# A two-layer hybrid transformer block on Trainium2: the norms' statistics products emitted later and pinned in TensorE's order

## The chip, the cores and the metric

The kernel runs on one core of one Trainium2 chip. The metric is the device time of one execution in microseconds (us). TensorE is called PE below, its weight loads PEld, VectorE DVE, ScalarE ACT, GpSimd POOL, and the queue that issues the transfers SP. The three executions shown of the kernel before took 3201.49, 3206.51 and 3210.8 us.

## What is computed

Two layers over 1024 latent tokens and 256 context tokens of width 1024, in float32. The reference, cut to what matters here:

```python
def rmsnorm(x, g):
    xf = x.astype(jnp.float32)
    y = xf * lax.rsqrt(jnp.mean(xf * xf, axis=-1, keepdims=True) + EPS)
    return y.astype(x.dtype) * g
...
def trunk_layer(x, xc, mod, mod_c, p, ang_row, ang_col, last):
    ...
    h = rmsnorm(x, p["g_pre_mix"]) * (1 + sc1) + sh1
    hc = rmsnorm(xc, p["g_pre_mix"]) * (1 + sc1c) + sh1c
    u = h @ w_in
    ...
    y = jnp.concatenate([y_sc, y_mla, y_cf, y_na], axis=-1) @ p["w_out"]
    x = x + ga1 * rmsnorm(y, p["g_post_mix"])
    ...
    hm = rmsnorm(x, p["g_pre_mlp"]) * (1 + sc2) + sh2
    x = x + ga2 * rmsnorm(sq_relu_mlp(hm, p["w_mlp1"], p["w_mlp2"]), p["g_post_mlp"])
```

The four mixers are a short convolution, latent attention (MLA), a Conformer convolution with a layer norm, and neighbourhood attention. The second layer leaves the context tokens' own output out.

## The kernel before

Activations lie transposed, 128 features on the partitions and tokens along the free axis, in three segments (`SEGS`): latent tokens 0 to 511, latent 512 to 1023, context 256. A float32 product is made as three float32r products (`mm3`, L117 to L124) of a high and a low half, which ACT and DVE or POOL split off (`hilo`, L93 and L94).

A norm needs, for each token, the sum of squares over 1024 features, which lie on eight tiles and 128 partitions. ACT squares (L133, L210, L229 or L863), DVE adds the squares up (`fold`, L145 and L148), and `rstd` (L151 to L174) does the rest:

- the statistics products, L161: for each 128 tokens one product of the accumulated squares with a column of ones, into one or two to four columns of a PSUM bank;
- the square root on ACT (L164), the reciprocal on DVE (L165), and DVE's product of the identity with it (L167);
- the broadcast product, L170, which spreads the factors of up to 512 tokens over all partitions in the same bank;
- a copy to SBUF by ACT (L173), except for norms with `ptag="O"`, which keep the bank.

`modulate` (L176 to L194) then makes the input of a projection from it (DVE L192, ACT L193, DVE L194), and `norm` (L200 to L236) the residual step (DVE L223 and L225) and, where another norm follows, that one's squares and its `modulate`. Both are generators: they yield a cost after each piece.

PSUM has banks under four tags: G (two), S (three), T (two), O (one). Products that ask for "R" get S or G in rotation. In the attention stage of segment 0 the rotation is G alone, so that projections and the Conformer's statistics share the two G banks, while attention has S, T and O.

The order of the work comes from two places. `merge` (L954) interleaves generators: it runs a main one and lets the others spend `rate` cost units for each unit of the main one (`RATES`, L33). This gives the order in which instructions are written. A list scheduler then sets each engine's queue at build time: by its own estimate of when operands are there it may put an instruction ahead of earlier ones of its engine. On the chip each queue runs in that fixed order.

In `layer` (L973) the stages are: projections with the Conformer convolution; MLA's projections; `atta`, the attention of segment 0, merged with the remaining projections (`rest`) and `cf_post` (L407), whose layer norm uses `rstd` with tag G; the output projection of segment 0 (`outproj`, L849) merged with the first norm of `y0` and attention of the other segments (`attb`); the second half's norm `n2` merged with `attb` at rate `od`; the MLP (`mlp`, L871) of segment 0 with the rest of `attb`; the output projections and norms of `y1` and, in layer 0, of `y2` (256 context tokens); and the MLP of segments 1 and 2, whose products on the context wait for `y2`'s norm (`ready`, L909). Norms of `y1` and `y2` use tag O, with one bank.

Two switches stand in the way of this flow: `PD and next(n2)` and `next(nb)` emit the first piece of a norm, its statistics included, before the stage that it is merged with. `stats` (L1107) runs a generator's first two pieces.

```python
    def merge(main, *others):
        ...
        for c in main:
            done += c
            for i, (g, rate) in enumerate(others):
                while live[i] and spent[i] < done * rate:
                    ...
                        spent[i] += next(g)
```

Of the kernel before, what the change touches and what calls it, by code (L numbers as in the profile page):

```python
# [4 lines left out]
F32 = mybir.dt.float32  # L5
# [7 lines left out]
P = 128  # L13
# [11 lines left out]
NA_SCALE = 64 ** -0.5  # L25
NEG = -1e30
HB = 2
QTAG = 'xl'
PA, PD = 0, 1
WALT = (3, 2)  # L30
MPE, RM, MX = 7, 1.0, 4
ROT0, ROT1, ROT2 = 'SGSGS', 'SGSGS', 'SGSGS'
# [29 lines left out]
class Kern:  # L62
# [88 lines left out]
    def rstd(self, accs, width, n, ptag, tag="e2", keep=False):  # L151

        nc = self.nc
        nt = n // P
        ps = self.ps(ptag)
        for t in range(nt):
            for i, a in enumerate(accs):  # L160
                nc.tensor.matmul(ps[:, t:t + 1], a[:, t * P:(t + 1) * P], self.ones[:, 0:1], start=i == 0,  # L161
                                 stop=i == len(accs) - 1)
        r = self.t([P, 12], "sm")[:, :nt]
        nc.scalar.activation(r, ps[:, :nt], AF.Sqrt, bias=self.eps, scale=1.0 / width)  # L164
        nc.vector.reciprocal(r, r)  # L165
        s = self.t([P, nt, P], tag)
        nc.vector.tensor_tensor(s, self.ident[:, None, :].to_broadcast([P, nt, P]),  # L167
                                r[:, :, None].to_broadcast([P, nt, P]), op=ALU.mult)
        s = s.rearrange("p t c -> p (t c)")
        nc.tensor.matmul(ps[:, :n], self.ones, s, start=True, stop=True)  # L170
        if keep:
            return ps[:, :n]
        nc.scalar.activation(s, ps[:, :n], AF.Copy)  # L173
        return s  # L174

    def modulate(self, get, n, l, which, v, H, o, acc=None, ptag="R", tag="e2", tmp=None):  # L176

        nc = self.nc
        if acc is None:
            acc = self.sumsq([lambda k=k: get(k) for k in range(KT)], n, tag)
            yield n / 60
        rs = self.rstd([acc], D, n, ptag, tag, ptag == "O")
        yield n / 100
        A, sh = self.gains(l, "A" + which, v), self.gains(l, "s" + which, v)
        for k in range(KT):
            x = get(k)
            hi, lo = (h.k(k)[:, o:o + n] for h in (H() if callable(H) else H))  # L190
            t = self.ps(tmp)[:, :n] if tmp else x
            nc.vector.scalar_tensor_tensor(t, x, A[:, k:k + 1], rs, op0=ALU.mult, op1=ALU.mult)  # L192
            nc.scalar.activation(hi, t, AF.Identity, bias=sh[:, k:k + 1])  # L193
            nc.vector.scalar_tensor_tensor(lo, t, sh[:, k:k + 1], f32(hi), op0=ALU.add, op1=ALU.subtract)  # L194
            yield n / 400
# [4 lines left out]
    def norm(self, y, si, o, n, l, which, acc, xsrc, xdst, nxt=None, ptag="R", tag="e2", tmp=None):  # L200
# [6 lines left out]
        if acc is None:  # L207
# [2 lines left out]
                nc.scalar.activation(q, y.tiles[k // y.kk][:, k % y.kk:k % y.kk + 512 // n, o:o + n], AF.Square)  # L210
                acc = self.fold(acc, q, 512 // n, n, tag)
            yield n / 60
        rs = self.rstd([acc], D, n, ptag, tag, ptag == "O")
        yield n / 100
        acc = None
        g = 512 // n
# [15 lines left out]
        if nxt:  # L232
            l2, w2, H = nxt
            yield n / 200
            yield from self.modulate(yk, n, l2, w2, v, H, o, acc, ptag, tag, tmp)


    def mod_pe(self, load):
# [168 lines left out]
    def cf_post(self, l, segs):  # L407
# [5 lines left out]
        for si in segs:  # L413
            o, n = SEGS[si]
            cs = [cfy[j][:, o:o + n] for j in range(2)]
            ps = self.ps("R")[:, :n]
            for j in range(2):
                nc.tensor.matmul(ps, self.ones, cs[j], start=j == 0, stop=j == 1)
            yield 4.0
            sqs = []  # L420
            for c in cs:
                nc.vector.scalar_tensor_tensor(c, ps, -1.0 / 256, c, op0=ALU.mult, op1=ALU.add)
                q = self.t([P, n], "e2")
                nc.scalar.activation(q, c, AF.Square)
                sqs.append(q)
            yield 5.0
            rs = self.rstd(sqs, 256, n, "G")
            yield 8.0
            zs = []
            for j, c in enumerate(cs):  # L430
                nc.vector.tensor_tensor(c, c, rs, op=ALU.mult)
                nc.scalar.activation(c, c, AF.Silu, scale=vec[:, V_LNG + j:V_LNG + j + 1],
                                     bias=vec[:, V_LNB + j:V_LNB + j + 1])
            yield 3.0
            for j, c in enumerate(cs):
                zh = self.t([P, n], "ge", F32R)
                zl = self.t([P, n], "ge", F32R)
                self.hilo(zh, zl, c)
                zs.append((zh, zl))
            for m in range(2):  # L440
                po = self.ps("R")[:, :n]
                self.mm3(po, [(wh(2 * j + m), wl(2 * j + m), zs[j][0], zs[j][1])
                              for j in range(2)])
                nc.scalar.activation(cs[m], po, AF.Copy)
            yield 4.0
# [54 lines left out]
    def mla_project(self, l, H, segs, qsegs):  # L500
# [4 lines left out]
        def ckv(si, ps):  # L505
            o, n = SEGS[si]
            c = self.t([P, n], "e2")
            nc.scalar.activation(c, ps, AF.Copy)
            rs = self.rstd([self.sumsq([lambda: c], n)], P, n, "R")
            nc.vector.scalar_tensor_tensor(c, c, vec[:, V_GKV:V_GKV + 1], rs, op0=ALU.mult, op1=ALU.mult)  # L510
            self.hilo(nh[:, o:o + n], nl[:, o:o + n], c)

# [6 lines left out]
    def mla_heads(self, l, qsegs):  # L519
# [21 lines left out]
        wh, wl = self.weights(self.a["wuq"][l], D)  # L541
        for si in qsegs:
            o, n = SEGS[si]
            rs = self.rstd([self.sumsq([lambda j=j: cq[j][:, o:o + n] for j in range(2)], n)], 256, n, "R")
            yield n / 100
            qh, ql = self.t([P, 2, n], "ah", F32R), self.t([P, 2, n], "ah", F32R)
            for j in range(2):
# [425 lines left out]
    def layer(self, l, H, pend):  # L973
# [50 lines left out]
        self.merge(self.outproj(l, 0, 0, 256, y0), (attb, R['ob']))  # L1024
        HM[0] = self.newh(512)
        na = self.norm(y0, 0, 0, 256, l, "1", self.acc, xsrc, self.scr["XM"], (l, "2", HM[0]))
        PA and next(na)
        self.merge(self.outproj(l, 0, 256, 256, y0), (na, R['on']), (attb, R['oc']))
        self.walt = 0
        n2 = self.norm(y0, 0, 256, 256, l, "1", self.acc, xsrc, self.scr["XM"], (l, "2", HM[0]))  # L1030
        PD and next(n2)
        self.merge(ch(na, n2), (attb, R['od']))
        m0 = self.mlp(l, (0,), HM, "s", {0: "s"}, None)
        self.merge(self.upto(m0, "tail"), (attb, R['mb']))
# [12 lines left out]
        self.merge(self.outproj(l, 1, 256, 256, y1), (nb, 1.5))  # L1047
        self.go(nb)
        nb = self.norm(y1, 1, 256, 256, l, "1", self.acc, xsrc, self.scr["XM"], (l, "2", HM[1]), **free)
        next(nb)  # L1050
        if not last:
            for m in (0, 2, 1, 3):
                self.ysplit(2, m, "c5")
            y2 = Seg(self.pools["s"], 256, F32, "s", self.nm("yo"))
            self.merge(self.outproj(l, 2, 0, 256, y2), (nb, R['pm']))
            self.go(nb)
            HM[2] = self.newh(256)
# [5 lines left out]
        if last:  # L1063
# [2 lines left out]
            self.merge(self.upto(m, "part"), (resa, R['pr']))  # L1066
            self.go(resa)
            nb = self.norm(self.macc[1], 1, 0, 256, l, "2", None, self.scr["XM"], xout, **free)
            self.stats(nb)
            n2 = self.norm(self.macc[1], 1, 256, 256, l, "2", None, self.scr["XM"], xout, tag="pt", tmp="T")  # L1070
            self.go(m)
            self.stats(n2)
            self.go(nb, n2)
            return None
        vecs = self.mod_vectors(("c5", "ah"))
# [15 lines left out]
        hn = hn()  # L1091
        self.merge(self.upto(m, "part"), (nb, R['mn']), (hn, R['mc']))
        self.go(nb, hn)
        p1 = self.norm(self.macc[1], 1, 0, 512, l, "2", None, self.scr["XM"], xout, (1, "1", lambda: HN[1]), **free)
        self.stats(p1)
        self.merge(m, (p1, R['mt']))
        HN[1], HN[2] = self.newh(512), self.newh(256)
        pend = ch(p1, self.norm(self.macc[2], 2, 0, 256, l, "2", None, self.scr["XM"], xout, (1, "1", HN[2]), **free))
        return HN, pend

    def turn(self, rot):
# [2 lines left out]
        yield 0.0  # L1104

    @staticmethod
    def stats(g):  # L1107

        next(g)
        next(g)  # L1110

    def upto(self, m, mark):

# [174 lines left out]
```

## Time and profile before

| what | value |
|---|---|
| runs | 3201.49, 3206.51, 3210.8 us (median 3206.51) |
| the profiled execution | 3201.57 us, of it the span from first to last instruction 3199.6 us |
| PE busy | 2959.4 us (92%), mean granted clock 0.961 |
| PEld, DVE, ACT, POOL busy | 2534.7, 2019.0, 1399.5, 1076.6 us |
| HBM | 127 GB/s over the span |

Busy shares are averages over stages with different limits. Times below are us from the span's start; a row of the timeline merges neighbours of one kind and ends, in brackets, with the idle time of its engine before it and what ended it.

### The profile page before, as it was taken

The page shows a single profiled execution, that of the slowest core. Times are in us where ns is not written, and L with a number is a line of the kernel's source. Part 1 is how long each engine was busy: PE and PEld are TensorE (multiplying, and loading weights), DVE is VectorE, ACT ScalarE, POOL GpSimd, SP SyncE. Part 2 cuts the span into 40 slices and gives each one's busy share as a digit, 9 for nine tenths or more (in the row PEclk, how much of TensorE's full clock was granted, in tenths as well). Part 3 has the DMA queues.
Part 4 walks back from the last instruction along what each step waited for, and adds up shares of the span by engine and source line. Part 5 has one row for each costly group of instructions (what it writes and reads, how often), then busy time and mean ns, then how long its engine had stood idle before and what let it go on. Part 6 is the DMA issues. An engine that isn't in the chain of part 4 may idle for free.

```text
span 3199.6 us, 46244 instructions
## 1 busy us (share of the span) xinstructions
PE 2959.4 (92%) x15916; PEld 2534.7 (79%) x15916; DVE 2019.0 (63%) x4128; ACT 1399.5 (44%) x2882; POOL 1076.6 (34%) x861
## 2 busy tenths in 40 slices
PE   7879889979999989889999998998989999989997
PEld 5767668878888878768888887777878888978886
DVE  8999556685753377975543689556776633654335
ACT  3313445666553364212322443555765433543332
POOL 2302122225444432223333421222334444334443
PEclk9889889989999989999999999998989999999998
DMA  7435423453533354563212443425445333534233
GB/s 264 152 120 189 118 62 101 126 148 107 159 109 96 102 186 150 193 213 107 91 60 66 145 140 126 141 76 144 151 116 146 111 96 96 172 100 147 96 97 104
DMA packets 284461, 410.01 MB, mean 128 GB/s; under 512 B 28098, under 2 KB 129474, under 8 KB 284228
## 3 DMA queue, kind: packets, MB, share of 16 engines
q1 hardware_dynamic: 284228, 407.07, 40.9%
q8 instruction: 126, 2.06, 0.3%
q14 instruction: 107, 0.88, 0.1%
HBM read 354.66 MB, written 52.30 MB: 127 GB/s over the span
## 4 chain that ended last, share of the span: by engine, by line
PE 70%; DVE 9%; DMA 5%; ACT 2%; issue 2%; SPq 1%; POOL 0%; DVEq 0%; ACTq 0%; POOLq 0%
PE G L122 11%; PE G L123 11%; PE G L124 11%; PE S L122 9%; PE S L124 9%; PE S L123 9%; PE T L675 3%; DMA xl<-in_wmodt_dram 2%; PE O L688 1%; PE O L687 1%; DVE xl L288 1%; DMA ah<-KR 1%; PE S L809 1%; PE S L758 1%; PE S L759 1%
## 5 line engine op out<-in xcount | busy, mean ns | idle before, releaser
L94 POOL TENSOR_TENSOR wl<-raw,wh 128x512 fp32r<-128x512 f32 x672 | 898.4, 1340 | 1525.7 <-ACT wh L93 1399.1
L93 ACT ACTIVATE wh<-raw 128x512 fp32r<-128x512 f32 x768 | 483.0, 631 | 847.7 <-PE S L123 391.9
L122 PE MATMUL G<-h,wh 128*128 128x512 f32 (+1 forms) x1128 | 427.0, 379 | 6.5 <-ACT h L193 2.3
L123 PE MATMUL G<-h,wh 128*128 128x512 f32 (+1 forms) x1128 | 423.0, 375 | 4.4 <-DVE h L194 4.3
L124 PE MATMUL G<-h,wl 128*128 128x512 f32 (+1 forms) x1128 | 423.4, 375 | 0.2 <-POOL wl L94 0.2
L122 PE MATMUL S<-h,wh 128*128 128x512 f32 (+1 forms) x904 | 324.6, 359 | 2.9 <-ACT h L193 1.6
L124 PE MATMUL S<-h,wl 128*128 128x512 f32 (+1 forms) x904 | 324.7, 360 | 1.4 <-POOL wl L94 1.4
L123 PE MATMUL S<-h,wh 128*128 128x512 f32 (+1 forms) x904 | 323.7, 358 | 0.0
L659 POOL TENSOR_SCALAR ah<-ah,sm 128x1280 f32<-128x1280 f32 (+3 forms) x144 | 148.2, 1033 | 410.4 <-DVE sm L658 155.2
L929 DVE TENSOR_TENSOR ac<-ac,S 128x512 f32<-128x512 f32 (+1 forms) x340 | 208.9, 617 | 114.6 <-PE S L124 113.7
L122 PEld LDWEIGHTS G<-h,wh 128*128 128x128 f32 x1128 | 215.7, 191 | 46.0 <-ACT h L193 4.7
L123 PEld LDWEIGHTS G<-h,wh 128*128 128x128 f32 x1128 | 215.2, 191 | 42.2 <-DVE h L194 6.0
L124 PEld LDWEIGHTS G<-h,wl 128*128 128x128 f32 x1128 | 215.4, 191 | 36.4 <-issue 0.7
L94 DVE TENSOR_TENSOR pt<-T,pt 128x512 fp32r<-128x512 f32 (+1 forms) x280 | 169.3, 615 | 87.9 <-ACT pt L93 86.6
L929 DVE TENSOR_TENSOR ac<-ac,G 128x512 f32<-128x512 f32 (+1 forms) x268 | 169.0, 631 | 82.1 <-PE G L124 80.9
L93 ACT ACTIVATE pt<-T 128x512 fp32r<-128x512 f32 (+1 forms) x280 | 146.5, 543 | 117.5 <-PE T L675 103.4
L122 PEld LDWEIGHTS S<-h,wh 128*128 128x128 f32 x904 | 173.9, 192 | 29.5 <-ACT h L193 2.3
L124 PEld LDWEIGHTS S<-h,wl 128*128 128x128 f32 x904 | 173.6, 192 | 27.3 <-POOL wl L94 2.7
L123 PEld LDWEIGHTS S<-h,wh 128*128 128x128 f32 x904 | 173.9, 192 | 25.6
L122 PE MATMUL G<-s,wh 128*128 128x512 f32 (+1 forms) x534 | 185.3, 348 | 2.2 <-ACT ge L863 1.7
L124 PE MATMUL G<-s,wl 128*128 128x512 f32 (+1 forms) x534 | 182.0, 341 | 3.3 <-DVE wl L94 3.2
L123 PE MATMUL G<-s,wh 128*128 128x512 f32 (+1 forms) x534 | 182.0, 341 | 0.3 <-DVE s L94 0.3
(339 smaller groups left out, 6938.9 us busy)
## 6 DMA issues: line engine op xcount, KB each, us to landing
raw<-in_w_dram SPq DMA_DIRECT2D x520, 256.0 KB, 2.6
xl<-in_wmodt_dram SPq DMA_DIRECT2D x160, 256.0 KB, 3.0
raw<-in_wout_dram SPq DMA_DIRECT2D x144, 256.0 KB, 3.0
raw<-in_win_dram SPq DMA_DIRECT2D x96, 256.0 KB, 3.1
ah<-KN SPq DMA_DIRECT2D x32, 320.0 KB, 4.9
ah<-MV SPq DMA_DIRECT2D x16, 640.0 KB, 6.4
ah<-NV SPq DMA_DIRECT2D x16, 640.0 KB, 4.9
XM<-yo SPq DMA_DIRECT2D x36, 256.0 KB, 2.9
```

The costliest lines, as they stand in the source:

```text
L93: nc.scalar.activation(hi, src, AF.Copy)
L94: (eng or nc.vector).tensor_tensor(lo, src, f32(hi), op=ALU.subtract)
L122: nc.tensor.matmul(out, wh, xh, start=i == 0, stop=False)
L123: nc.tensor.matmul(out, wh, xl, start=False, stop=False)
L124: nc.tensor.matmul(out, wl, xh, start=False, stop=i == last)
L288: nc.vector.scalar_tensor_tensor(q, w, 1.0, vecs[v][h], op0=ALU.mult, op1=ALU.mult, accum_out=dst)
L659: nc.gpsimd.tensor_scalar(p[:, :L], p[:, :L], sm[:, 9:10], 1.0, op0=ALU.mult, op1=ALU.mult)
L675: nc.tensor.transpose(T[:, i, q * P:(q + 1) * P], ps_list[q][:, cols[q]:cols[q] + P], self.ident)
L687: nc.tensor.matmul(O[:, a:b], V[:, kt, :], th[:, i, a:b], start=first, stop=False)
L688: nc.tensor.matmul(O[:, a:b], V[:, kt, :], tl[:, i, a:b], start=False, stop=last)
L758: nc.tensor.matmul(S, Qt[:, 0, q:q + P], K[0][:, ks], start=True, stop=False)
L929: nc.vector.tensor_tensor(a, a, ps, op=ALU.add)
```

## The change

`rstd` becomes a generator. It yields `LEAD` = 6.0 units before it takes its PSUM bank and emits the statistics products, and `MID` = 3.0 units before the broadcast product. So in a merge other work is written between the squares and the statistics, and between statistics and broadcast. `pin` wraps both products: the scheduler must keep each behind the last PE instruction that was written before it; later ones may still go ahead of it. At three sites (`cf_post`, MLA's key/value norm, MLA's query norm) `value` runs the generator through without a break, so there only the pin is new. The early pieces (`PA`, `PD`, `next(nb)`) are gone; `stats` runs four pieces instead of two; the tail of the last layer merges the first half's norm with the last products; `y2` moves from the pool `s` to the pool `ah`; and `p1` and its successor keep tag `e2` instead of `pt`.

```diff
+LEAD, MID = 6.0, 3.0
-PA, PD = 0, 1
...
     def rstd(self, accs, width, n, ptag, tag="e2", keep=False):
...
         nt = n // P
+        yield LEAD
         ps = self.ps(ptag)
         for t in range(nt):
             for i, a in enumerate(accs):
-                nc.tensor.matmul(ps[:, t:t + 1], a[:, t * P:(t + 1) * P], self.ones[:, 0:1], start=i == 0,
-                                 stop=i == len(accs) - 1)
+                self.pin(nc.tensor.matmul(ps[:, t:t + 1], a[:, t * P:(t + 1) * P], self.ones[:, 0:1], start=i == 0,
+                                          stop=i == len(accs) - 1))
...
-        nc.tensor.matmul(ps[:, :n], self.ones, s, start=True, stop=True)
+        yield MID
+        self.pin(nc.tensor.matmul(ps[:, :n], self.ones, s, start=True, stop=True))
...
-        rs = self.rstd([acc], D, n, ptag, tag, ptag == "O")
+        rs = yield from self.rstd([acc], D, n, ptag, tag, ptag == "O")
...
+    def pin(self, ins):
+
+        return self.tc.keep_in_program_order(ins)
...
-            rs = self.rstd(sqs, 256, n, "G")
+            rs = self.value(self.rstd(sqs, 256, n, "G"))
...
-            rs = self.rstd([self.sumsq([lambda: c], n)], P, n, "R")
+            rs = self.value(self.rstd([self.sumsq([lambda: c], n)], P, n, "R"))
...
-        PA and next(na)
...
-        PD and next(n2)
...
-        next(nb)
         if not last:
...
-            y2 = Seg(self.pools["s"], 256, F32, "s", self.nm("yo"))
+            y2 = Seg(self.pools["ah"], 256, F32, "ah", self.nm("yo"))
...
-            self.stats(nb)
+            next(nb)
             n2 = self.norm(self.macc[1], 1, 256, 256, l, "2", None, self.scr["XM"], xout, tag="pt", tmp="T")
-            self.go(m)
-            self.stats(n2)
+            self.merge(m, (nb, 1.5))
+            self.go(nb)
             self.go(nb, n2)
...
-        p1 = self.norm(self.macc[1], 1, 0, 512, l, "2", None, self.scr["XM"], xout, (1, "1", lambda: HN[1]), **free)
-        self.stats(p1)
+        p1 = self.norm(self.macc[1], 1, 0, 512, l, "2", None, self.scr["XM"], xout, (1, "1", lambda: HN[1]), ptag="O", tmp="T")
+        next(p1)
```

How PE's queue changes at three places. First, `cf_post` in the attention stage of layer 0, where the Conformer's layer norm takes its statistics (bank `G_3964`) of segment 1. L675, L687, L688 and L758 to L760 are attention's products; L122 to L124 on a G bank are projections. Before:

```order
L123 MATMUL G_3800<-h_3_399,wh_3581 128x512
L124 MATMUL G_3800<-h_3_395,wl_3582 128x512
L161 MATMUL G_3964<-ones,e_3827 128x1
L161 MATMUL G_3964<-ones,e_3830 128x1
L161 MATMUL G_3964<-ones,e_3827 128x1
L161 MATMUL G_3964<-ones,e_3830 128x1
L161 MATMUL G_3964<-ones,e_3827 128x1
L758 MATMUL S_3450<-ah_3287,xl_3445 128x512
L687 MATMUL O_3176<-pt_3234,ah_2938 128x256
```

Now (lines from 155 on have moved down, attention's by six):

```order
L765 MATMUL S_3947<-ah_3929,xl_3934 128x256
L766 MATMUL S_3947<-ah_3926,xl_3934 128x256
L162 MATMUL G_3964<-ones,e_3827 128x1
L162 MATMUL G_3964<-ones,e_3830 128x1
L162 MATMUL G_3964<-ones,e_3827 128x1
L162 MATMUL G_3964<-ones,e_3830 128x1
L162 MATMUL G_3964<-ones,e_3827 128x1
L162 MATMUL G_3964<-ones,e_3830 128x1
L162 MATMUL G_3964<-ones,e_3827 128x1
L162 MATMUL G_3964<-ones,e_3830 128x1
L693 MATMUL O_3857<-pt_3863,ah_3641 128x256
L122 MATMUL G_4074<-h_0_400,wh_3575 128x256
```

The statistics stand behind 194 attention products that came after them before, and no projection stands among those 194: the next one on a G bank is the last row shown.

Second, the norm of `y1`'s second half in layer 0, which runs beside the output projection of `y2` (L122 to L124 on `c`). Before, the broadcast of the first statistics (L170) and the statistics of the second (L161) are neighbours:

```order
L124 MATMUL S_11907<-c_11642,wl_11904 128x256
L161 MATMUL O_11620<-ones,ma_11237 128x1 x2
L170 MATMUL O_11620<-pt_11626,ones 128x256
L161 MATMUL O_11772<-ones,pt_11696 128x1 x2
L170 MATMUL O_11772<-pt_11778,ones 128x256
L122 MATMUL S_11948<-c_11639,wh_11938 128x256
```

Now there are 42 products between the first two and 101 between the next two:

```order
L123 MATMUL G_11948<-c_11630,wh_11938 128x256
L162 MATMUL O_11719<-ones,ma_11237 128x1 x2
L124 MATMUL G_11948<-c_11630,wl_11939 128x256
...
L123 MATMUL S_11997<-c_11633,wh_11993 128x256
L172 MATMUL O_11719<-pt_11725,ones 128x256
L124 MATMUL S_11997<-c_11633,wl_11994 128x256
```

Third, the norm of `y2` just after, beside the first MLP products of segment 1 (L122 to L124 on `h`, second half of its columns). Before, 138 products stand between its broadcast `O_12085` (not shown) and the statistics that follow it:

```order
L124 MATMUL S_12491<-h_3_11194,wl_12428 128x256
L161 MATMUL O_12234<-ones,pt_12119 128x1 x2
L122 MATMUL S_12491<-h_3_11194,wh_12427 128x256
L123 MATMUL S_12491<-h_3_11198,wh_12427 128x256
L124 MATMUL S_12491<-h_3_11194,wl_12428 128x256
L170 MATMUL O_12234<-pt_12240,ones 128x256
L122 MATMUL G_12521<-h_0_12059,wh_12350 128x256
```

Now there is none:

```order
L122 MATMUL S_12463<-h_3_11194,wh_12384 128x256
L123 MATMUL G_12426<-h_3_11198,wh_12317 128x256
L124 MATMUL G_12426<-h_3_11194,wl_12318 128x256
L123 MATMUL S_12463<-h_3_11198,wh_12384 128x256
L124 MATMUL S_12463<-h_3_11194,wl_12385 128x256
L172 MATMUL O_12137<-pt_12143,ones 128x256
L162 MATMUL O_12418<-ones,pt_12215 128x1 x2
L172 MATMUL O_12418<-pt_12424,ones 128x256
L122 MATMUL G_12521<-h_0_12059,wh_12311 128x256
```

## Rows read from the trace of the kernel before

**Rows 1.** The page: busy time, then PE and its clock in 40 slices.
```profile
PE 2959.4 (92%) x15916; PEld 2534.7 (79%) x15916; DVE 2019.0 (63%) x4128; ACT 1399.5 (44%) x2882; POOL 1076.6 (34%) x861
...
PEclk9889889989999989999999999998989999999998
```

**Rows 2.** PE's waits before statistics products: us in total, times, longest.
```profile
PE O L161 <- DVE pt L148: 19.0, 3, 9.9
PE O L161 <- DVE e L148: 14.0, 1, 14.0
PE S L161 <- ACT e L133: 11.3, 3, 5.4
PE S L161 <- DVE e L148: 8.3, 3, 5.0
PE S L161 <- DVE pt L148: 7.1, 1, 7.1
PE O L161 <- DVE T L192: 1.9, 2, 1.1
```

**Rows 3.** Timeline of PE at the first norm (start, us, work, idle before).
```profile
53.41 1.83 PE L161 MATMUL O<-ones,e 128*128 128x1 f32 x8 [13.98 <-DVE e L148]
56.17 0.80 PE L375 MATMUL S<-h,wh 128*128 128x512 f32 x1 [0.93 <-ACT h L193]
```

**Rows 4.** Windows: length, PE, PEld, DVE, ACT, POOL busy (count), PEclk, DMA, GB/s.
```profile
0.00:320.00 320.00, 262.73 (x1266) 217.07 (x1266) 301.88 (x687) 98.63 (x193) 63.41 (x46) 0.94 0.54 181
```

**Rows 5.** Windows: attention's products alone on PE, five stretches.
```profile
430.80:479.90 49.10, 36.62 (x181) 29.77 (x181) 25.70 (x64) 25.12 (x56) 9.39 (x7) 0.83 0.34 78
581.70:606.40 24.70, 19.15 (x91) 15.44 (x92) 15.71 (x40) 14.06 (x37) 5.05 (x5) 0.84 0.40 93
2102.30:2124.80 22.50, 16.87 (x104) 13.43 (x102) 15.98 (x41) 18.57 (x39) 5.40 (x4) 1.00 0.15 41
2172.20:2185.80 13.60, 9.56 (x67) 8.22 (x65) 11.35 (x26) 9.11 (x20) 1.96 (x4) 0.99 0.66 197
2194.00:2249.90 55.90, 42.64 (x233) 36.22 (x231) 36.34 (x102) 32.80 (x86) 12.82 (x17) 0.85 0.46 123
```

**Rows 6.** Windows: short attention runs amid projections, then a mixed stretch.
```profile
399.50:403.20 3.70, 3.70 (x27) 3.43 (x26) 1.98 (x5) 3.29 (x10) 1.34 (x1) 1.00 0.00 0
881.20:888.40 7.20, 6.34 (x49) 5.77 (x48) 6.79 (x18) 4.76 (x12) 1.50 (x2) 1.00 0.34 100
486.20:580.80 94.60, 92.60 (x583) 83.26 (x582) 59.86 (x142) 54.29 (x122) 26.39 (x28) 0.98 0.40 118
```

**Rows 7.** Windows: attention alone on PE while `y0`'s norms run, layers 0 and 1.
```profile
668.00:700.60 32.60, 18.26 (x84) 15.37 (x83) 27.15 (x62) 20.38 (x47) 7.01 (x5) 0.69 0.28 87
2312.90:2347.90 35.00, 23.87 (x118) 20.14 (x117) 30.36 (x73) 21.95 (x52) 8.23 (x6) 0.76 0.52 143
```

**Rows 8.** Timeline of PE, second half of `y1`, layer 0.
```profile
1176.20 1.19 PE L170 MATMUL O<-pt,ones 128*128 128x256 f32 x2 [1.78 <-DVE pt L167]
1186.11 0.99 PE L161 MATMUL O<-ones,pt 128*128 128x1 f32 x4 [8.72 <-DVE pt L148]
1188.20 1.19 PE L170 MATMUL O<-pt,ones 128*128 128x256 f32 x2 [1.10 <-DVE pt L167]
1191.06 0.58 PE L122 MATMUL S<-c,wh 128*128 128x256 f32 x1 [1.66 <-ACT ma L863]
```

**Rows 9.** Windows: the two stretches behind that wait.
```profile
1180.00:1190.00 10.00, 2.18 (x6) 1.43 (x6) 6.95 (x18) 2.29 (x6) 0.00 (x0) 0.50 0.67 210
1190.00:1200.00 10.00, 8.94 (x58) 8.94 (x59) 9.39 (x21) 8.77 (x25) 2.59 (x2) 0.72 0.15 46
```

**Rows 10.** Timeline of PE, norm of `y2` in layer 0: statistics, broadcast, first reader.
```profile
1235.10 0.50 PE L161 MATMUL O<-ones,pt 128*128 128x1 f32 x4
...
1237.53 0.67 PE L170 MATMUL O<-pt,ones 128*128 128x256 f32 x2 [1.47 <-DVE pt L167]
1239.29 0.39 PE L122 MATMUL G<-h,wh 128*128 128x256 f32 x1 [1.09 <-ACT h L193]
```

**Rows 11.** Timeline of PE, second half of `y1` in layer 1.
```profile
2811.45 0.59 PE L170 MATMUL O<-pt,ones 128*128 128x256 f32 x2
2821.97 0.99 PE L161 MATMUL O<-ones,pt 128*128 128x1 f32 x4 [9.92 <-DVE pt L148]
```

More of the change, by code (lines that the diff above doesn't have):

```diff
@@ L212, in norm @@
             yield n / 60
-        rs = self.rstd([acc], D, n, ptag, tag, ptag == "O")
+        rs = yield from self.rstd([acc], D, n, ptag, tag, ptag == "O")
         yield n / 100
@@ L543, in mla_heads @@
             o, n = SEGS[si]
-            rs = self.rstd([self.sumsq([lambda j=j: cq[j][:, o:o + n] for j in range(2)], n)], 256, n, "R")
+            rs = self.value(self.rstd([self.sumsq([lambda j=j: cq[j][:, o:o + n] for j in range(2)], n)], 256, n, "R"))
             yield n / 100
@@ L1093, in layer @@
         self.go(nb, hn)
-        p1 = self.norm(self.macc[1], 1, 0, 512, l, "2", None, self.scr["XM"], xout, (1, "1", lambda: HN[1]), **free)
-        self.stats(p1)
+        p1 = self.norm(self.macc[1], 1, 0, 512, l, "2", None, self.scr["XM"], xout, (1, "1", lambda: HN[1]), ptag="O", tmp="T")
+        next(p1)
         self.merge(m, (p1, R['mt']))
         HN[1], HN[2] = self.newh(512), self.newh(256)
-        pend = ch(p1, self.norm(self.macc[2], 2, 0, 256, l, "2", None, self.scr["XM"], xout, (1, "1", HN[2]), **free))
+        pend = ch(p1, self.norm(self.macc[2], 2, 0, 256, l, "2", None, self.scr["XM"], xout, (1, "1", HN[2]), ptag="O", tmp="T"))
         return HN, pend
@@ L1106, in stats, with value @@
     @staticmethod
-    def stats(g):
-        next(g)
-        next(g)
+    def stats(g, n=4):
+        for _ in range(n):
+            next(g)
+    @staticmethod
+    def value(g):
+        while True:
+            try:
+                next(g)
+            except StopIteration as e:
+                return e.value
     def upto(self, m, mark):
```

## The prediction

> **What bounds the kernel.** I read the page first. PE is busy for 2959.4 of 3199.6 us and the next engine, DVE, for 2019.0; the weight loads lie beside the products [rows 1]. So the time is PE's work plus PE's idle time, 240 us, plus what a lowered clock adds. An edit that only reorders PE can change nothing but those two parts. Next I read PE's waits before the statistics products: the six groups add up to 61.6 us [rows 2], and that sum is the most that a better place for these products can take off directly. Then I read the stretches where the order changes.
>
> At the first norm the wait of 13.98 us ends on DVE, and the product that needs the norm's result follows 2.8 us later, after its own wait on ACT [rows 3]; DVE is busy for 301.88 of the first 320 us [rows 4]. PE is not the limit there. In the attention stages the reader should compare prices per product. Where only attention is on PE, 676 products take 165.8 us in five stretches, .245 each; the single prices are .271, .271, .216, .203 and .240 [rows 5]. PE is idle for a quarter of such a stretch and the clock is .83 to .85 in the three dearer ones. Where attention comes in short runs amid projections, 76 products take 10.9 us, .143 each, at full clock and with hardly any idle time; the mixed stretch costs .162 for a product of either kind [rows 6]. So an attention product costs about .1 us less when a projection stands near it. Nearly the whole forecast hangs on this difference, because the change moves statistics products behind long rows of attention and everything that needs the same bank waits with them.
>
> **The change, part by part.** Each part is given as a difference in PE's time, with bounds.
>
> *Waits that stay.* The waits of the projections' and MLA's norms (nearly all of the 11.3 and 8.3 us on S banks [rows 2]), the 9.92 us of layer 1's second half [rows 11] and the 7.1 us of the tail keep their neighbours in PE's order: the call is run through without a break there, or nothing else is left to put between. With the 9.9 and the 7.1 that is some 36 of the 61.6 us. 0.
>
> *First norm.* Its statistics now follow 84 other products, so the wait of 13.98 us [rows 3] is filled. What ends it is DVE, which has 18.1 us free in 320 [rows 4], and the next projection waits for DVE and ACT as before. PE gets ahead with products that it would make later anyway, and waits later. I take 0; the bounds are -14 (the whole wait) and +2.
>
> *Layer 0, `atta`.* Before, the scheduler had lifted the statistics over 194 attention products. Now they stay behind these, and as `G` has two banks that projections share, no projection can run meanwhile. The attention-only runs were 180 and 90 products (49.10 + 24.70 = 73.8 us [rows 5]); they become 203 and 196, 129 more, which before ran amid projections at .143: 73.8 + 18.4 = 92.2 us. After: the first at this stage's own .271, 55.0 us; the second at the mean, .245, 48.0 us; together 103.0. **+10.8**; at .216 throughout -6, at .271 throughout +16.
>
> *Layer 0, norms of `y0`.* The attention-only run beside them grows from 76 to 228 products. Before: 32.60 us [rows 7] and 152 x .143 = 21.7, together 54.3. After, the price .245 gives 55.9 us. DVE gives about the same: attention takes .155 us of DVE for a product (105.1 us in 676 [rows 5]), so the norms' own DVE time is 27.15 - 76 x .155 = 15.4, and 228 x .155 + 15.4 plus the 5.4 us in which DVE was free before is 56.2. **+1.9**; at .216 it is -5, at the 35.00/118 = .297 that a run beside norms cost in layer 1 [rows 7] it is +13.
>
> *Layer 1, `atta`.* Runs of 101 and 64 products (22.50 + 13.60 = 36.1 us [rows 5]) become 115, 92 and 70, together 277 or 112 more. Before: 36.1 + 112 x .143 = 52.1. After, at this stage's own .216: 59.8. **+7.7**; at .203 it is +4, at .271 +23.
>
> *Layer 1, norms of `y0`.* 108 products become 121 and 36. Before: 35.00 [rows 7] + 49 x .143 = 42.0. After, by DVE: 157 x .155 = 24.3, the norms 30.36 - 108 x .155 = 13.6, and the 4.6 us free before: 42.6. **+0.6**; at .216 it is -8, at .297 it is +5.
>
> *Layer 0, `y1` and `y2`.* Of the second half of `y1`, the waits 1.78, 8.72 and 1.10 and the 1.66 before its reader [rows 8] go, 13.3 us. The clock behind them recovers too: 2.18 us of PE at .50 and 8.94 at .72 [rows 9] would take 1.1 and 2.5 less at full clock. At `y2` the waits 1.47 and 1.09 [rows 10] go. Off: 13.3 + 3.6 + 2.6 = 19.5. But the residual step and the second statistics of `y2` had 138 products as cover and now have none: those products are emitted earlier, and what comes after them reads `y2`'s own result. The nearest rows are the same place of `y1`, 8.72 and 9.92 [rows 8, 11]; I take 9.9. Its broadcast waits 1.1, its reader 1.4 (between 1.09 and 1.66), the clock again costs 3.6, and `y1`'s reader, now 7 products behind its broadcast, may still wait 1.7. On: 17.7. **-1.8**; if something covers `y2` it is -18, if the clock stays low for a stretch more it is +4.
>
> *The rest.* Layer 1's first half of `y1` keeps 12 products between statistics and broadcast: 0, at worst +3, two waits like the 1.47 and 1.78 above. With a norm move its square root on ACT, reciprocal and product on DVE, its squares, and on SP its loads of `x` and stores of `XM`; no wait in rows 8, 10 or 11 ended on a transfer, and PE's statistics are the link that these follow, so I add nothing; without that cover a late load would lengthen the `y2` wait. The new pool of `y2` and tag of `p1` change buffers alone: 0.
>
> **Sum.** 10.8 + 1.9 + 7.7 + 0.6 - 1.8 = +19.2. The profiled execution took 3201.57 us, so 3220.8; the median of the runs stands 4.9 above it, which gives **3226 us**.
>
> The pages bear on one term. The clock in the three dear runs cost 36.62 x .17 + 19.15 x .16 + 42.64 x .15 = 15.7 us of 165.8 [rows 5], or .023 for a product. The Trainium skill, "TensorE: Matmul & The Clock Gate", section "The HAM clock gate (the "warmup" mystery)", says that for modelling the ramp's penalty is below 1% of a span and no cold count should be fitted. Followed literally it would price the new runs at .257 - .023 = .234, and the sum would come to about +1, 3208 us; the rows show the clock low in each run that is as long as the new ones, so they decide. The same notes' "Perfetto Trace Analysis", section "Optimization Strategy", advise to interleave regimes that contend for different engines; the change does the opposite in `atta`, and the trace agrees, .143 against .245.
>
> **The rivals.** The four runs hold 784 products in all but layer 1's `atta` (399 + 228 + 157) and took 188.5 us before; at a common price p the total is 784 p - 188.5 + 5.9. My terms amount to p = .257.
>
> *A, faster: attention alone is no dearer than in layer 1.* DVE and ACT work ahead in the long runs and PE seldom waits, so p is .203 to .216, as the two runs of 104 and 67 products show [rows 5]. Then the change is -27 (layer 1's `atta` at .203 too) to -13, 3180 to 3193 us, 3189 as its middle weighted to the longer run. It decides below p = .221, where the total passes -9.6. Against it: all three longer or earlier runs cost .24 or more. Chance 0.22.
>
> *B, no change: the clock holds.* If the long runs keep the full clock as layer 1's two short ones did (1.00 and .99 [rows 5]), p is .234 and the total +1: 3208 us. The same figure to 5 us comes out if `y2`'s wait is covered after all, 3226 - 15 = 3211. Against it: .83, .84 and .85 in the others. Chance 0.22. This is what the rule on the ramp amounts to.
>
> *C, the change doesn't do what it says.* For 36 of 61.6 us of waits that is so in every case, and at the first norm the statistics leave a queue that wasn't the limit. It bounds what A can gain and has no time of its own.
>
> **Numbers.** Forecast 0.56, A 0.22, B 0.22. A difference of 0.3%, 9.6 us, is about what a measurement of this kernel can tell from no change; it lies at p = .245 above and .221 below. So faster 0.23 (A and the forecast's low tail), same 0.22, slower 0.55. Within the forecast the terms' bounds, which need not fall together, give 3204 to 3248. The range takes in A down to its low price, 3180, and above it the case that two terms stand at their dear ends (`atta` of layer 1 and the norms of `y0`, +26 over the sum): 3252.
>
> **What would show it.** In the changed profile: two attention-only runs of some 200 products in layer 0's `atta`, each 48 to 55 us with a clock near .84; one of about 230 beside `y0`'s norms, near 56 us; at the second half of `y1` in layer 0 no wait above 2 us before statistics, and one of 9 to 10 us at `y2`'s; the waits of 5.4, 5.0, 9.9 and 7.1 us [rows 2] still there; the first projection near 56 us still waiting for ACT. I am wrong if the long runs cost under .221 a product, if projections stand among them after all, or if PE's total idle time falls by more than 10 us.

## The result and the profile after

The changed kernel takes 3286.74 us (median of 4 runs, 3283.68 to 3299.01) against 3204.7 for the kernel before beside it: 1.0261 of its time, with an interval of 1.023 to 1.0292, or 82 us more. The sign was forecast, the size was not: 3226 us, and 3252 at most. The profiled execution took 3299.01 us, the slowest of the four; a second profile of the same kernel is among the experiments.

Two lines of the page answer to [rows 1]:

```profile
PE 3008.1 (91%) x15916; PEld 2568.2 (78%) x15916; DVE 2024.8 (61%) x4128; ACT 1406.9 (43%) x2887; POOL 1087.8 (33%) x861
...
PEclk9799888979999999999999999998979999989998
```

The span grew from 3199.6 to 3297.2 us. Of these 97.6 us PE was busy for 48.7 more, with the same 15916 products, and idle for the other 48.9. So half of the loss is the same work at a lower clock, and half is waiting.

PE's waits, in total, times and longest, as in [rows 2]:

```profile
PE S L764 <- ACT ah L658: 19.5, 18, 3.6
...
PE O L162 <- DVE pt L148: 18.9, 2, 9.6
PE S L381 <- ACT h L195: 16.6, 1, 16.6
...
PE G L162 <- DVE e L148: 10.8, 2, 10.6
...
PE G L172 <- DVE e L168: 7.7, 1, 7.7
```

The 14.0 us at the first norm are now 16.6 us at the projection behind it, which waits for ACT until 56.55 as forecast. Layer 1's wait at `y1` is still 9.25 us, and the 8.72 us of layer 0 [rows 8] are now 9.60 us at `y2`. In PE's timeline (start, us, work, idle before), `y1`'s second half and `y2`'s:

```profile
1246.43 0.51 PE L162 MATMUL O<-ones,pt 128*128 128x1 f32 x4
...
1274.23 0.99 PE L162 MATMUL O<-ones,pt 128*128 128x1 f32 x4 [9.60 <-DVE pt L148]
```

Next the stages, by PE's own milestones: the last query projection of MLA, the last output projection of `y0`, the first MLP product of segment 0. Windows of the kernel before, from the first milestone to the second, layer 0 and layer 1 (columns as in [rows 4]):

```profile
356.40:668.20 311.80, 284.39 (x1747) 250.00 (x1746) 192.12 (x445) 187.60 (x421) 78.92 (x68) 0.94 0.40 109
2021.70:2313.10 291.40, 262.90 (x1592) 229.64 (x1592) 186.68 (x425) 175.09 (x400) 73.80 (x66) 0.96 0.42 120
```

Then from the second milestone to the third:

```profile
668.20:700.60 32.40, 18.06 (x82) 15.19 (x81) 27.15 (x62) 20.18 (x47) 7.01 (x5) 0.69 0.27 87
2313.10:2347.90 34.80, 23.67 (x116) 19.94 (x116) 30.16 (x73) 21.75 (x52) 8.23 (x6) 0.75 0.52 142
```

The changed kernel, the same four:

```profile
358.50:685.00 326.50, 295.56 (x1769) 261.51 (x1768) 196.72 (x443) 187.08 (x429) 81.92 (x71) 0.91 0.36 99
2060.90:2385.20 324.30, 287.65 (x1638) 248.94 (x1637) 188.41 (x431) 178.63 (x413) 81.69 (x70) 0.91 0.40 110
685.00:756.40 71.40, 49.50 (x237) 41.80 (x236) 51.45 (x124) 39.58 (x90) 10.47 (x11) 0.71 0.46 124
2385.20:2438.40 53.20, 28.03 (x129) 22.88 (x128) 37.39 (x89) 26.42 (x61) 6.70 (x5) 0.69 0.31 95
```

The attention stage with the output projection is longer by 14.7 us in layer 0 and 32.9 in layer 1, with 22 and 46 more products in it; the stretch from there to the first MLP product, 32.4 and 34.8 us before, by 39.0 and 18.4. The MLP of segment 0 gives 17.9 back in layer 0, since more attention is already done (1894 products on PE for 2069). The start adds 2.1, `y1` and `y2` of layer 0 add 1.4. The last 7 us arise after layer 1's first MLP product; no experiment followed them up. So nearly everything lies in the attention stages and beside `y0`'s norms.

The attention-only runs came as the order said. The two of layer 0's `atta`, 195 products at .271 and 192 at .238:

```profile
413.90:466.70 52.80, 40.30 (x213) 34.87 (x212) 29.95 (x73) 21.89 (x58) 9.94 (x8) 0.81 0.33 75
503.00:548.80 45.80, 34.88 (x203) 29.91 (x201) 29.79 (x77) 24.84 (x61) 11.09 (x16) 0.85 0.54 155
```

Beside `y0`'s norms, 220 products took 71.5 us, .325 each instead of .247; in layer 1's `atta` 107 and 84 took 31.8 and 24.1 us, .297 and .287 instead of .216.

### The profile page after: what moved, and what is told of

Read it like the earlier page. It is cut to its first block, busy times and chain, and to the rows that moved or that the text cites. A ratio compares the mean times of both kernels' runs of the same rounds, so it can differ in the third digit from the quotient of the medians.

```text
span 3297.2 us, 46274 instructions
## 1 busy us (share of the span) xinstructions
PE 3008.1 (91%) x15916; PEld 2568.2 (78%) x15916; DVE 2024.8 (61%) x4128; ACT 1406.9 (43%) x2887; POOL 1087.8 (33%) x861
## 5 line engine op out<-in xcount | busy, mean ns | idle before, releaser
L122 PE MATMUL G<-h,wh 128*128 128x512 f32 (+1 forms) x1104 | 422.8, 383 | 8.8 <-ACT h L195 4.0
L123 PE MATMUL G<-h,wh 128*128 128x512 f32 (+1 forms) x1104 | 418.9, 380 | 11.1 <-DVE h L196 10.8
L124 PE MATMUL G<-h,wl 128*128 128x512 f32 (+1 forms) x1104 | 417.2, 378 | 0.0
L122 PE MATMUL S<-h,wh 128*128 128x512 f32 (+1 forms) x928 | 336.0, 362 | 2.0 <-ACT h L195 1.6
L124 PE MATMUL S<-h,wl 128*128 128x512 f32 (+1 forms) x928 | 333.6, 360 | 1.7 <-POOL wl L94 1.7
L123 PE MATMUL S<-h,wh 128*128 128x512 f32 (+1 forms) x928 | 333.2, 359 | 0.0
L665 POOL TENSOR_SCALAR ah<-ah,sm 128x1280 f32<-128x1280 f32 (+3 forms) x144 | 161.2, 1123 | 478.7 <-DVE sm L664 217.2
L122 PEld LDWEIGHTS G<-h,wh 128*128 128x128 f32 x1104 | 215.0, 195 | 48.8 <-ACT h L195 7.1
L124 PEld LDWEIGHTS G<-h,wl 128*128 128x128 f32 x1104 | 214.7, 195 | 35.2
L122 PEld LDWEIGHTS S<-h,wh 128*128 128x128 f32 x928 | 178.7, 193 | 29.8 <-ACT h L195 2.3
L124 PEld LDWEIGHTS S<-h,wl 128*128 128x128 f32 x928 | 177.7, 192 | 28.5 <-POOL wl L94 2.8
L123 PEld LDWEIGHTS S<-h,wh 128*128 128x128 f32 x928 | 178.2, 192 | 27.5 <-issue 1.0
L905 DVE TENSOR_TENSOR S<-S,ge 128x512 f32<-128x512 f32 (+1 forms) x80 | 48.0, 600 | 223.8 <-ACT ge L901 223.8
L122 PE MATMUL G<-s,wh 128*128 128x256 f32 (+1 forms) x520 | 182.4, 352 | 2.7 <-DVE ac L935 1.0
L681 PE MATMUL T<-ident,ah 128*128 128x128 f32 x976 | 171.9, 298 | 13.6 <-POOL ah L665 13.5
```

What stands on the lines that cost most here:

```text
L122: nc.tensor.matmul(out, wh, xh, start=i == 0, stop=False)
L123: nc.tensor.matmul(out, wh, xl, start=False, stop=False)
L124: nc.tensor.matmul(out, wl, xh, start=False, stop=i == last)
L665: nc.gpsimd.tensor_scalar(p[:, :L], p[:, :L], sm[:, 9:10], 1.0, op0=ALU.mult, op1=ALU.mult)
L681: nc.tensor.transpose(T[:, i, q * P:(q + 1) * P], ps_list[q][:, cols[q]:cols[q] + P], self.ident)
L905: nc.vector.tensor_tensor(ps, ps, r, op=ALU.mult)
```

## The experiments

All were run beside the kernel before; "over before" is the difference of medians in one comparison.

**The parts of the change.** The first four separate the pin, the units and the early pieces. *The pin alone*, on the kernel before:

```diff
-                nc.tensor.matmul(ps[:, t:t + 1], ...)
+                self.tc.keep_in_program_order(nc.tensor.matmul(ps[:, t:t + 1], ...))
-        nc.tensor.matmul(ps[:, :n], self.ones, s, start=True, stop=True)
+        self.tc.keep_in_program_order(nc.tensor.matmul(ps[:, :n], self.ones, s, start=True, stop=True))
```

> The kernel before with the pin alone: statistics and broadcast products are kept behind the PE instruction written before them; no units are yielded ahead of them, and the early pieces stay. PE's order then has the attention-only runs of the changed kernel in the stages atta (194 and 192 products in layer 0; 107, 84 and 75 in layer 1), and short ones beside the norms of y0 (56; 65 and 25). Theory P (the pin in atta costs what the changed kernel lost there, some 15 us in layer 0 and 19 in layer 1, and the rest of the loss, at the norms of y0, needs the units too): 3205 + 34 = about 3239 us. Rival U (the loss comes from the 9 units that each norm gives to the work merged with it, wherever its products stand): about 3205 us, within 0.3% of before. Rival S (the loss is that of the early pieces that were taken away): about 3205 us too.

3233.0 us, 27 over before (1.0086, 1.0067 to 1.0105): less than P's 34, and far from U and S. The same windows as above:

```profile
358.80:669.10 310.30, 280.38 (x1747) 247.96 (x1746) 196.59 (x445) 186.55 (x424) 79.43 (x69) 0.95 0.39 111
2013.60:2320.10 306.50, 273.64 (x1592) 236.80 (x1591) 186.69 (x425) 175.91 (x403) 75.13 (x66) 0.93 0.41 115
```

With the same products in each, layer 0 needs 1.5 us less although its long runs are there, and layer 1 needs 15.1 us more, 10.7 of them PE's busy time at a lower clock. The two runs of layer 0:

```profile
414.40:465.00 50.60, 37.85 (x212) 32.05 (x211) 29.98 (x73) 21.90 (x57) 9.98 (x8) 0.87 0.34 78
499.80:545.30 45.50, 34.01 (x203) 29.05 (x201) 29.47 (x77) 24.96 (x61) 11.12 (x16) 0.89 0.55 157
```

The term for layer 0's `atta` has fallen.

*No pin*, in the changed kernel:

```diff
-        return self.tc.keep_in_program_order(ins)
+        return ins
```

> The changed kernel without the pin: units and the taken-away early pieces as they are, the scheduler free to lift the statistics. PE's order has the attention-only runs of before in atta, and 162 products beside the norms of y0 in layer 0 (220 with the pin, 70 before), 100 and 25 in layer 1 (113 and 35 with the pin, 100 before). P: atta's 34 us go, and of the 59 us lost at y0's norms (21 and 38) something between a third and two thirds: 3225 to 3245 us. U and S: the loss stays, 3275 to 3290 us.

3238.07 us, 32 over before (1.0103): P's range.

*No units*:

```diff
-LEAD, MID = 6.0, 3.0
+LEAD, MID = 0.0, 0.0
```

> The changed kernel with LEAD and MID at 0, so that the pin and the taken-away early pieces remain. atta's long runs stay; beside y0's norms 119 and then 71 products in layer 0, 109 in layer 1. P: the 34 us of atta stay, and the y0 stages lose less than with units, 10 to 30 us instead of 59: 3250 to 3270 us. U: 3205 us. S: 3275 to 3290 us.

3265.71 us, 60 over before (1.0192, 1.0171 to 1.0212), as P had it. The units cost 22 us with the pin. Without the pin, units and missing early pieces together cost only the 32.

*The Conformer unpinned*, in the changed kernel:

```diff
-            rs = self.value(self.rstd(sqs, 256, n, "G"))
+            rs = self.value(self.rstd(sqs, 256, n, "G", on=False))
```

> The changed kernel with the pin left out for the Conformer's statistics alone (its two products in each of cf_post's calls). atta then has the runs of before (179 and 90; 100 and 64), and beside y0's norms 209 and 113 and 26 stay. P: the 34 us of atta are back: 3287 - 34 = 3253 us. U and S: within 5 us of the changed kernel, 3282 to 3292 us.

3271.16 us, 16 less than the changed kernel, half of what P said; U and S had 5 at most. The runs of `atta` are those of before, so a price per product in a row overstates what they cost.

**Where the pin and the early pieces act.** *The rest only*: `cf_post` unpinned, `y0`'s norms unpinned and without units, early pieces back:

```diff
+        next(n2)
         self.merge(ch(na, n2), (attb, R['od']))
```

> The changed kernel with the Conformer's statistics and the norms of y0 put back: no pin and no units there, and the first pieces of y0's second norm emitted early again. PE's attention-only runs are those of before (179 and 90, 70, 25, 48; 100 and 64, 215, 101). What is left of the change is pin, units and order at y1, y2, the tail and the norms between the layers. Theory P2 (all of the loss arises in atta and beside y0's norms): within 8 us of before, 3198 to 3214 us. Rival R (the rest costs something that the attention stages hide or pass on): over 3220 us.

3220.85 us, 18 over before (1.0052): R, by a hair, though little of the extra time is where the changed kernel lost it. By the milestones, 11 of the 19 us of this profile arise after layer 1's first MLP product and 5 before the first milestone of layer 0. The last kernel of this section leaves room for 6 us of it in the changed kernel's loss.

*The early pieces off*, one flag in the kernel before:

```diff
-PA, PD = 0, 1
+PA, PD = 0, 0
```

> The kernel before with one flag changed: the first pieces of y0's second norm are no longer emitted before the merge. No pin, no units. By the three runs so far the pin with the pieces taken away (no units) lost 59 us and the pin with them kept 27. Theory S2 (without the early pieces the two norms stand one after the other, and the time from the last output projection to the first MLP product grows from 32 to over 50 us in layer 0, without help from pin or units): 3220 to 3240 us. Rival I (the early pieces matter only where the pin holds the later ones back): 3200 to 3212 us. PE's order has 86 attention products beside y0's norms in layer 0 (70 before) and 109 in layer 1 (100 before), which speaks for I.

3230.03 us, 27 over before (1.0085, 1.0062 to 1.0107): S2's size without pin or units. Its picture was wrong for layer 0: up to the first MLP product only 34.9 us pass, not 50, and the loss comes behind it; in layer 1 it is 42.1 us. Two windows of it, to the first MLP product and behind:

```profile
670.90:705.80 34.90, 20.73 (x99) 17.76 (x97) 29.20 (x69) 22.66 (x53) 7.75 (x7) 0.67 0.28 86
705.80:750.00 44.20, 39.30 (x232) 35.27 (x233) 27.22 (x64) 25.61 (x63) 13.14 (x10) 0.91 0.31 84
```

The MLP starts on the first half and then waits for the second (4.1 us on DVE's `h`).

*`y0`'s norms unpinned* (`on=False` for `na` and `n2`), the changed kernel otherwise:

> The changed kernel with the pin left out at the norms of y0 alone; the units stay and the pin in atta stays. Attention-only runs beside those norms: 177 (220 with the pin) and 100 (113 and 35). If pin and units simply add: no pin anywhere gave 3238, the Conformer's pins are worth 16 (the changed kernel less the one without them), so 3254 us. If the pin at y0's norms costs nothing by itself: 3287 us.

3261.49 us, 25 less than the changed kernel; 7 off the sum.

*The pin in layer 0 alone*, on the kernel before (`self.pinned = l == 0`):

> The kernel before with the pin in layer 0 alone, early pieces kept, no units. In the profile with the pin everywhere, layer 0 ended 8 us sooner than before and layer 1 lost 32. Theory L (the pin as such is harmless or useful where the run beside y0's norms stays as short as before, and what it costs arises in layer 1's atta): 3195 to 3203 us, no slower than before. Rival C (the 8 us were the clock of one execution, and 194 and 192 attention products in a row cost what their price says): 3210 to 3218 us.

3197.54 us against 3202.76 (0.9984, 0.9974 to 0.9993): L. The two long runs of layer 0 cost nothing, and the pin there even gains 5 us. So the pin's 32 us are all layer 1's.

**Which of layer 1's pins.** *Pin everywhere but at layer 1's Conformer* (`on=l == 0` in `cf_post`), then *without `y0`'s norms of layer 1 too*:

> The kernel before with the pin everywhere but at layer 1's Conformer statistics. The pin in layer 0 alone gave 5 us less than before, the pin in both 27 more, so layer 1's pins cost 32. In the profiles 15 of these had arisen by the end of y0's output projection, and the rest beside y0's norms and after. Theory A1 (the Conformer's pins in layer 1's atta cost 15, the pins of y0's norms there the rest): 3233 - 15 = 3218 us. Rival A2 (what is lost at y0's norms is only passed on from atta, whose attention is then further on or further back): 3197 to 3203 us.

> As the kernel with the pin everywhere but at layer 1's Conformer statistics, and the norms of y0 in layer 1 unpinned too. The pin stays at MLA's norms, at y1, y2 and the tail of both layers and everywhere in layer 0. A1 and A2: the same as with the pin in layer 0 alone, 3194 to 3202 us. Rival T (layer 1's y1 or tail pays for the pin): over 3210 us.

3212.47 us (1.0035, 1.0025 to 1.0046) and 3198.97 us (0.9979, 0.997 to 0.9988). From 3233.0 the Conformer's pins of layer 1 are worth 20.5 us and those of `y0`'s norms there 13.5; A1 had 15 and 17; A2 had nothing for the second. The last kernel is 5.5 us faster than before. Its stages are back at 312.3 and 293.2 us. From the last output projection to the first MLP product it takes 27.7 and 34.9 us:

```profile
672.30:700.00 27.70, 17.38 (x84) 14.77 (x83) 25.85 (x64) 18.18 (x42) 6.44 (x5) 0.72 0.30 91
2308.20:2343.10 34.90, 23.88 (x118) 20.04 (x116) 30.25 (x73) 21.83 (x52) 8.26 (x6) 0.76 0.52 142
```

What the pin does at `y0`'s norms is a matter of one row. In these rows `ones,ma` are the first statistics of the second norm, `ones,e` the second ones of the first norm. PE's timeline before:

```profile
662.58 0.50 PE L161 MATMUL G<-ones,e 128*128 128x1 f32 x4
...
672.46 0.51 PE L161 MATMUL G<-ones,ma 128*128 128x1 f32 x4
...
2316.40 0.50 PE L161 MATMUL G<-ones,e 128*128 128x1 f32 x4
...
2317.51 0.61 PE L161 MATMUL G<-ones,ma 128*128 128x1 f32 x4
```

With the pin alone:

```profile
672.23 0.61 PE L162 MATMUL G<-ones,ma 128*128 128x1 f32 x4
...
2323.41 0.50 PE L162 MATMUL G<-ones,e 128*128 128x1 f32 x4
...
2344.64 0.50 PE L162 MATMUL G<-ones,ma 128*128 128x1 f32 x4
```

In layer 0 the second norm's first statistics stand where they stood. In layer 1 they were lifted over attention products and came 1.1 us after the first norm's second ones; pinned, they come 21.2 us after them, and the first MLP product moves from 34.8 to 46.2 us after the last output projection.

**The early pieces and the units, in the changed kernel.** *Early pieces back* (`self.stats(n2, 3)` before the merge), and *the changed kernel once more*:

> The changed kernel with one line put back: the second norm of y0 emits its first three pieces (its first statistics, their broadcast) before the merge, as before. Pin and units stay. Theory S2 (that norm's chain of statistics then runs beside the last output projections instead of after the first norm's; taking the pieces away alone cost 27 us): 3287 - 27 = about 3260 us, and the time from the last output projection to the first MLP product in layer 0 falls from 71 to under 50 us. Rival O (what counts is the number of attention products that PE's order puts in a row; they are 207 against 220 here in layer 0, and 129 against 113 in layer 1): 3278 to 3292 us.

> The changed kernel once more, for a second profile: the first one was of an execution of 3299 us, 12 above the median. All theories: 3280 to 3292 us; the same attention-only runs, of 71 us beside y0's norms in layer 0 and 53 in layer 1, to 3 us.

3273.54 us (1.0219) and 3295.2 us (two runs; 1.0284, 1.0266 to 1.0302). The second profile repeats the first, 70.8 and 53.2 us beside `y0`'s norms, at a median 3 us above what was expected. So the early pieces alone bring 13 to 22 us back, between S2 and O. But S2's picture was wrong: the second norm's first statistics do come early (683.04 us in layer 0, before the first norm's second ones at 705.22), and yet the stretches from the last output projection to the first MLP product stay as long as in the changed kernel:

```profile
677.30:748.20 70.90, 49.61 (x224) 40.34 (x224) 51.63 (x123) 37.57 (x85) 12.47 (x9) 0.69 0.43 120
2372.40:2425.20 52.80, 31.21 (x147) 24.25 (x145) 36.72 (x87) 31.44 (x65) 9.43 (x7) 0.74 0.47 133
```

Against the second profile, 11 of the 21 us are won after layer 1's first MLP product and 7 between layer 0's first MLP product and layer 1's attention; why, no run shows. Two more kernels show what the units hold.

*No units at `y0`'s norms* (`yield LEAD * units`, with `units=0.0` for `na` and `n2`), then *that with the early pieces back*:

> The changed kernel with the units taken away at y0's norms alone (both layers); pin everywhere, early pieces gone, units at all other norms. All units together cost 21 to 26 us with the pin (the changed kernel less the one without units) and 5 without it. Theory V (the units cost only beside y0's norms, where each of the four statistics steps in a row lets more attention in, and the pin then holds the statistics behind it): as without any units, 3262 to 3270 us. Rival W (the units cost elsewhere, at y1, y2 and between the layers): 3280 to 3292 us.

> As the kernel without units at y0's norms, and the early pieces of y0's second norm put back. The stage is then as in the kernel with the pin alone, and what differs from that (3233 us, 27 over before) is the rest of the change, worth 17 by the kernel that has only it. Theory V: 3233 + 17 = about 3250 us, so the early pieces are worth 15 to 27 us here as in the two pairs so far (18 and 27). Rival X (the early pieces help only where the pin does not hold them: nothing is gained): 3262 to 3270 us.

3264.85 us (1.0191, 1.0174 to 1.0207), the same as without any units: V, the units cost only there. Its attention stages hold the same products as before:

```profile
357.50:669.80 312.30, 283.79 (x1747) 251.77 (x1746) 196.29 (x445) 186.35 (x424) 79.59 (x69) 0.93 0.40 110
2048.80:2360.50 311.70, 277.53 (x1592) 240.62 (x1592) 185.27 (x425) 175.14 (x403) 76.46 (x66) 0.91 0.41 114
```

Layer 0 takes what it took before, and layer 1 20.3 us more. So 14.2 of the changed kernel's 14.7 us in layer 0's stage, and 12.6 of its 32.9 in layer 1's, come with the units at `y0`'s norms and the 22 and 46 products that they bring into it. Then 3235.65 us (1.0108, 1.0084 to 1.0133): the early pieces are worth 29 us once the units are out of their way, and what is left is the pin's 27 and some 6. V's 3250 was too high, because it added the 17 of the rest.

## Why the prediction was wrong

From the changed kernel to one faster than before, each step a run:

| kernel | us | step | last output projection to first MLP product, layers 0, 1 |
|---|---|---|---|
| changed | 3286.74 | | 71.4, 53.2 |
| no units at `y0`'s norms | 3264.85 | -22 | 54.5, 41.2 |
| and early pieces back | 3235.65 | -29 | 28.3, 46.7 |
| pin alone | 3233.0 | -3 | 28.1, 46.2 |
| no pin at layer 1's Conformer | 3212.47 | -20.5 | 28.2, 46.0 |
| nor at `y0`'s norms there | 3198.97 | -13.5 | 27.7, 34.9 |
| before | 3204.43 | +5.5 | 32.4, 34.8 |

The medians are from several comparisons, whose kernel before stood at 3202.8 to 3206.1 us; a step of 3 us means nothing. Each taken against the kernel before beside it, the steps are -20, -29, -6, -19, -13.5 and +5.5.

*Norms of `y0`, +1.9 and +0.6: this step failed.* Taken away in this order, units, early pieces and layer 1's pin at these norms are worth 22 + 29 + 13.5, some 65 us. I counted attention products and asked which engine would be full. None was: in the 71.4 us of layer 0 PE was busy for 49.5 and DVE for 51.5. Nor does the number of products set the time. Without any pin, 118 products take 50.8 us in layer 1, where 116 took 34.8 before:

```profile
2338.30:2389.10 50.80, 25.36 (x118) 21.35 (x115) 42.20 (x97) 26.38 (x63) 7.81 (x6) 0.66 0.48 136
```

What sets the end is four statistics in a row. A norm's second ones follow on ACT's and DVE's work with the result of its first. The second norm's first ones need nothing of the first norm, but now stand behind it in PE's queue. In the changed kernel:

```profile
699.63 0.50 PE L162 MATMUL G<-ones,e 128*128 128x1 f32 x4
...
724.85 0.85 PE L162 MATMUL G<-ones,ma 128*128 128x1 f32 x4
...
755.99 0.50 PE L162 MATMUL G<-ones,e 128*128 128x1 f32 x4
756.36 0.36 PE L122 MATMUL G<-h,wh 128*128 128x256 f32 x1
...
2396.10 0.61 PE L162 MATMUL G<-ones,e 128*128 128x1 f32 x4 [0.19 <-DVE e L148]
...
2411.80 0.50 PE L162 MATMUL G<-ones,ma 128*128 128x1 f32 x4
...
2437.56 1.01 PE L162 MATMUL G<-ones,e 128*128 128x1 f32 x4 [10.58 <-DVE e L148]
```

In layer 0 PE does not wait at any of these rows: attention products fill its queue up to them. In layer 1 the last one waits 10.58 us for DVE. Before, the second norm's first statistics came 10 us after the first norm's second ones in layer 0, and 1.1 us in layer 1; now 25.2 and 15.7 us. Before, the second norm ran beside the rest of the first; now it follows it, and the units put the first one itself later: in layer 0 its second statistics came 5.6 us before the end of the last output projection, and now come 14.6 us behind it. Without units at these norms, its second statistics come at 664.88 and the other two at:

```profile
697.76 0.50 PE L162 MATMUL G<-ones,ma 128*128 128x1 f32 x4
...
723.46 0.85 PE L162 MATMUL G<-ones,e 128*128 128x1 f32 x4
```

and with the early pieces too:

```profile
678.74 0.60 PE L162 MATMUL G<-ones,ma 128*128 128x1 f32 x4
...
702.86 0.85 PE L162 MATMUL G<-ones,e 128*128 128x1 f32 x4
```

In the five kernels that have the pin and no units at `y0`'s norms of both layers, the second norm's second statistics come 21 to 26 us after the later of two rows, the first norm's second statistics and the second norm's first, and the first MLP product follows within 1 us. So whatever delays either row delays the MLP. With the units in place it is not so regular (42.6 and 12.2 us with the early pieces back), and that part stays open. The front part showed that the early `next(n2)` goes; my sum had no term for it.

*`atta` of layer 0, +10.8: wrong.* Nothing by the pin alone (311.8 against 310.3 us). Its two runs took 96.1 us, 22.3 more than the 73.8 before, where I had 29.2 more. The rest of the stage shrank from 238.0 to 214.2 us with 143 products less, .166 each, close to the .162 of the mixed stretch [rows 6]; I had credited the products taken out of it with .143, the price of the short runs, 18.4 us in all. Both sides of the sum were off.

*`atta` of layer 1, +7.7: mis-sized.* The pin there is worth 20.5. I took this stage's own .216, from two runs at full clock; the new ones, in the changed kernel, were at .79 and .83 and cost .29.

*First norm, waits that stay, `y1` and `y2`: right.* 0 became +2; the `y2` wait is 9.60 us for 9.9; `y1` and `y2` came to +1.4 for -1.8. *The rest, 0:* 7 us appeared behind layer 1's first MLP product, and no run shows why.

*The rivals.* A and B both needed cheaper runs; neither came, and the clock in layer 0's two was .81 and .85. The point that I named for slower, .245 a product, was passed: the 755 products of the new runs at those places took 232.6 us, .308. The range failed with the step: its dear end for `y0`, .297, still was a price per product, and none for a longer chain.

## What to carry to other kernels

Before moving a norm's small products, draw its chain of dependent steps and see which other chain runs beside it; an early piece that looks like a leftover may be what makes two chains overlap. A pin holds only what the order around it would otherwise lift, so compare, for each place, where the row stood and now stands: in one layer the same pin moved nothing, in the other 20 us. And price work by whole stages with equal instruction counts, not by the runs within them.

## What was not expected of the hardware

The clock carries half of the loss: 48.7 of 97.6 us, 1.5% of the span, are busy time of the same products, at a mean granted clock of 0.946 against 0.961; the ratio of the two clocks would make it 46.9. In the two stretches beside `y0`'s norms, in which PE is idle for 21.9 and 25.2 us, it was .71 and .69. It had been as low there before, .69 and .75, but in stretches of 32.4 and 34.8 us instead of 71.4 and 53.2. I had called the rule on the ramp in the Trainium skill's "TensorE: Matmul & The Clock Gate", section "The HAM clock gate (the "warmup" mystery)", a way to a smaller sum. That section puts the ramp's penalty below 1% of a typical span. The 1.5% that the clock adds here, by one change alone, are above it.

What stays open is why the pinned runs kept their clock better in layer 0 (0.94 before, 0.95 pinned for the stage) than in layer 1 (0.96 and 0.93), and where the 18 us of the kernel with the rest only come from; by the ladder at most some 6 of them are in the changed kernel's loss.
